# A two-layer streaming encoder in float32 products: the low part of weights split ahead of use is made by ScalarE and an accumulating DMA instead of VectorE

## The chip, the cores and the metric

The kernel runs on one core of a Trainium2 chip. Its time is the device time of one execution in microseconds (us). A core has five engines with a queue of their own: TensorE (PE, with PEld for loading its weights), VectorE (DVE), ScalarE (ACT), GpSimd (POOL), and SyncE (SP), which here only issues DMAs. Every engine works through its queue in order; waits between engines are semaphores.

## The reference

A trunk of two layers on 656 tokens (16 learned tokens, a prompt of 512, and 8 running streams of 16 tokens) with 1024 channels, all in float32. Cut to what matters here, one layer is:

```python
h = rmsnorm(x, g_mix)
proj = h @ w_in                      # then attention, convolution and a recurrence on its parts
x = x + mix @ w_out
h2 = rmsnorm(x, g_ffn)
gate, val = split(h2 @ w_up, 2)      # 1024 -> 2 x 2816
gate_c = causal_dwconv(gate, ffn_past, ffn_conv_w, ffn_conv_b)     # width 3
x = x + (gelu(gate_c) * val) @ w_down
```

After the second layer, `y = rmsnorm(x, g_final)` is written for all tokens, besides caches and states.

## The kernel before, in words

Activations lie with channels on the 128 partitions and tokens along the row; a block of 128 channels is one tile (`x0` to `x7`). A float32 product is made of three matmuls of a shorter type (float32r): every operand is split into a high part, which is the rounded value, and a low part, which is what the rounding left. `mm3` (L373) multiplies high by high, high weights by low activations, and low weights by high activations, into one accumulator.

Weights come from HBM into one of four buffers `raw` (up to 512 KB, 8 blocks of 128 rows; `w_load`, L342, a DMA on SP's queue). `w_split` cuts each half of such a buffer (256 KB, 128x512 elements) into its parts: ScalarE writes the high part (L359), VectorE subtracts it from `raw` and writes the low part (L360). Most units go through four shared buffers each, `whi` and `wlo`, which come free when TensorE has used them. Some weights are split ahead of their use, and their parts lie in tiles of their own, `ghi` and `glo` (argument `own`): 37 halves in the whole program. They are

- 3 halves for the first input projection at the very start (here `start["on"]` holds);
- in each layer, 6 halves for the first three blocks of the up-projection, split during the output projection (blocks `e_u`, written as `w3` below);
- in each layer, 4 halves for the first gates that are computed after those blocks (`wg`; their products are `d_g`, two blocks of output rows, each in two column ranges c0 and c1);
- 6 halves for the first blocks of layer 1's input projection, split at the end of layer 0;
- 8 halves for the last part of the last down-projection (`wl`; products `d_fin`), one for each block of 128 output rows, named m0 to m7 below. There the tokens are taken in two column ranges, 384 columns first and 256 columns after, so that the norm and the output of the first range overlap the products of the second. The first three halves are split at the start of the stage, that of m+3 when block m has been added to the residual.

Around the first gates the stage works as follows. ScalarE writes `ga`, the last tap of the short convolution (L1086), VectorE adds the other taps (L1089), ScalarE applies the gelu (L1092), GpSimd multiplies by the norm's factors (L1231, L1232), and VectorE multiplies the value product into it (`gv`, L1236 to L1238). GpSimd also copies rows of past gates into `gp` (L1076) and rows for the output into `gout` (L1081, L1082). After the first gates, pairs of blocks are multiplied by a Strassen scheme with seven products in place of eight: its sums of weights are `wcb` (GpSimd, L960), split into `whi` (ScalarE, L966) and `wlo` (VectorE, L967); its sums of activations are `fh` (ScalarE L1063, VectorE L1064); its products `d_v` and `d_g` are taken out by VectorE at L992 and L996.

The order on each engine is not that of the source: a recording layer collects the instructions and places them by a planner, so a change of one helper moves others too. The tile names in the profile are those in the program, without buffer numbers.

Of the kernel before, what the change touches and what calls it, by code (L numbers as in the profile page):

```python
# [9 lines left out]
F32 = mybir.dt.float32  # L10
# [3 lines left out]
ALU = mybir.AluOpType  # L14
# [142 lines left out]
def trunk_kernel(ctx: ExitStack, tc: tile.TileContext, i: dict, o: dict, depth: int = 2):  # L157
# [12 lines left out]
    V, A, G, PE = nc.vector, nc.scalar, nc.gpsimd, nc.tensor  # L170
# [148 lines left out]
    start = {"on": False}  # L319

    def seq(ins):

        if start["on"]:
            tc.keep_in_program_order(ins)
            start[ins.ins.engine] = ins.ins
# [19 lines left out]
    def unit_s(name):  # L345
        return S(name, F32R)[:, :512].rearrange("p (k n) -> p k n", n=128)

    def w_split(raw, kt, a=0, own=False):

        half = 4 if kt in (4, 8) else 3  # L350
        units = []
        while a < kt:
            n = min(half, kt - a)
            if own:
                hi, lo = unit_s("ghi"), unit_s("glo")
            else:
                hi = wsp.tile([128, 4, 128], F32R, tag="whi", name="whi")
                lo = wsp.tile([128, 4, 128], F32R, tag="wlo", name="wlo")
            seq(A.copy(hi[:, :n], raw[:, a:a + n]))  # L359
            seq(V.tensor_tensor(out=lo[:, :n], in0=raw[:, a:a + n], in1=hi[:, :n].bitcast(F32), op=ALU.subtract))  # L360
            units += [(hi, lo, m) for m in range(n)]
            a += n
        return units

    def weights(w, k0, kt, own=False):
        return w_split(w_load(w, k0, kt), kt, 0, own)
# [744 lines left out]
    for l in range(depth):  # L1111
# [7 lines left out]
        if l == 0:  # L1119
            hs = []  # L1120
            nc.sync.dma_start(out=xs[0][:, :T], in_=i["x"][0])
            raws = [w_load(w[col[n]], 0, 8, ((0, 4),)) for n in range(3)]
            for m in range(1, 4):
                nc.sync.dma_start(out=xs[m][:, :T], in_=i["x"][m])
            for n in range(3):
                nc.sync.dma_start(out=raws[n][:, 4:], in_=w[col[n], :, 512:].rearrange("p (k n) -> p k n", n=128))
            for m in range(4, 8):
                nc.sync.dma_start(out=xs[m][:, :T], in_=i["x"][m])
            w3 = []
            start["on"] = True  # L1130
            for m in range(8):
                hs.append(split(xs[m], par("g_mix", m), f"h{l}{m}"))
                if m == 0:
                    w3 = [w_split(raws[n], 4) for n in range(3)]
                if m == 3:
                    w3 = [w3[n] + w_split(raws[n], 8, 4, True) for n in range(3)]
            for m in range(8):
                sq_add(m, E=V)
            start["on"] = False
# [88 lines left out]
        for ft in range(2):  # L1228
            ps = ps3[2] if ft == 0 else gemm(weights(wu[NFF + 1], 0, 8), ks8, hs, f"v{l}1", cx, PB)
            a, av = gates.pop(ft)  # L1230
# [168 lines left out]
```

## Time and profile before

| | |
|---|---|
| median of 3 runs | 1700.11 us (1699.21 to 1701.23) |
| the profiled execution | 1700.97 us, of which the span from the first to the last instruction is 1699.2 us |
| mean granted TensorE clock | 0.988 of full speed |
| TensorE busy | 1626.8 us, 96% of the span |
| VectorE busy | 1288.1 us, 76% |
| ScalarE busy | 843.3 us, 50% |
| GpSimd busy | 552.7 us, 33% |
| transfers issued by GpSimd | 40, 13.44 MB, 4.5% of the 16 DMA engines' time |

The profile is of one execution. The busy shares are averages over stages with different limits; a stage is read from the timeline and from the waits that end last in it. An engine's idle time is put down to the engine or DMA whose signal came last.

### The profile page before, as it was taken

To read this page: it belongs to the slowest core of one execution; us is meant where nothing else is said; L and a number is where in the kernel's file an instruction comes from. 1 tells how busy PE (TensorE), PEld (TensorE's weight loads), DVE (VectorE), ACT (ScalarE), POOL (GpSimd) and SP (SyncE) were. 2 spreads that over 40 slices of the span, in tenths; PEclk is the share of its full clock that TensorE was granted. 3 is DMA by queue.
4 is the path that set the end of the run, shared out by engine and by line. 5 is a ranking of instruction groups with operands and counts; after the bars stand their busy time and mean duration, and the time that the engine had idled before them with its cause. 6 is when DMAs were issued, how large, how long until landed. Compare 5 with 4: busy or idle time off the path is not lost.

```text
span 1699.2 us, 28519 instructions
## 1 busy us (share of the span) xinstructions
PE 1626.8 (96%) x10772; PEld 1530.0 (90%) x10772; DVE 1288.1 (76%) x2470; ACT 843.3 (50%) x1648; POOL 552.7 (33%) x626
## 2 busy tenths in 40 slices
PE   7999999998989999999999999999999999999997
PEld 6898878898989999999988988788899899999996
DVE  6579985769896696696747898856899867768765
ACT  6656576554553343343427556665544434334334
POOL 0102220017563353462201032100276534435413
PEclk9999999999999999999999999999999999999998
DMA  6236431341213322222412364314502232222212
GB/s 221 77 92 158 115 98 42 105 163 70 75 66 113 109 81 84 74 74 86 158 64 86 94 149 99 93 57 135 177 29 75 88 118 83 96 67 80 88 49 87
DMA packets 68090, 164.62 MB, mean 97 GB/s; under 512 B 11984, under 2 KB 17616, under 8 KB 67952
## 3 DMA queue, kind: packets, MB, share of 16 engines
q1 hardware_dynamic: 62192, 149.36, 26.8%
q0 software_dynamic: 5760, 13.44, 4.5%
q8 instruction: 84, 1.38, 0.3%
q14 instruction: 54, 0.44, 0.1%
HBM read 129.80 MB, written 19.54 MB: 88 GB/s over the span
## 4 chain that ended last, share of the span: by engine, by line
PE 74%; DVE 16%; issue 4%; ACT 2%; POOL 2%; DMA 1%; SPq 0%; DVEq 0%; ACTq 0%; POOLq 0%
PE d_i L373 16%; PE d_dn L373 16%; PE d_v L373 10%; PE d_g L373 8%; PE d_oa L373 5%; DVE wlo L967 3%; DVE lo_g L332 2%; PE e_i L373 2%; PE e_u L373 2%; PE sc L490 2%; PE hl L784 1%; DVE ga L1089 1%; PE d_fin L373 1%; PE po L526 1%; DVE fh L1064 1%
## 5 line engine op out<-in xcount | busy, mean ns | idle before, releaser
L373 PE MATMUL d_v<-fh,whi 128*128 128x328 f32 (+1 forms) x1120 | 252.1, 312 | 1.3 <-ACT whi L966 1.3
L359 ACT CAST whi<-raw 128x384 fp32r<-128x384 f32 (+2 forms) x243 | 132.7, 548 | 239.7 <-PE d_i L373 76.4
L373 PE MATMUL d_g<-fh,whi 128*128 128x328 f32 (+1 forms) x1008 | 226.6, 312 | 0.0
L373 PE MATMUL d_i<-hi_h,whi 128*128 128x328 f32 x672 | 219.2, 326 | 0.0
L373 PE MATMUL d_i<-lo_h,whi 128*128 128x328 f32 x672 | 213.8, 318 | 0.0
L373 PE MATMUL d_i<-hi_h,wlo 128*128 128x328 f32 x672 | 212.8, 317 | 0.0
L373 PE MATMUL d_dn<-hi_g,wlo 128*128 128x328 f32 (+1 forms) x640 | 199.2, 312 | 6.1 <-DVE wlo L360 6.1
L373 PE MATMUL d_dn<-lo_g,whi 128*128 128x328 f32 (+1 forms) x640 | 199.0, 311 | 0.0
L373 PE MATMUL d_dn<-hi_g,whi 128*128 128x328 f32 (+1 forms) x640 | 198.4, 311 | 0.0
L360 DVE TENSOR_TENSOR wlo<-raw,whi 128x384 fp32r<-128x384 f32 (+2 forms) x243 | 164.3, 689 | 40.1 <-ACT whi L359 32.2
L373 PEld LDWEIGHTS d_v<-fh,whi 128*128 128x128 f32 x1120 | 189.2, 189 | 1.6 <-ACT whi L966 1.6
L373 PE MATMUL d_v<-fh,wlo 128*128 128x328 f32 (+1 forms) x560 | 176.5, 315 | 7.2 <-DVE wlo L967 6.5
L966 ACT CAST whi<-wcb 128x512 fp32r<-128x512 f32 x152 | 94.0, 619 | 164.1 <-PE d_dn L373 66.5
L373 PEld LDWEIGHTS d_g<-fh,whi 128*128 128x128 f32 x1008 | 170.2, 189 | 0.0
L373 PE MATMUL d_g<-fh,wlo 128*128 128x328 f32 (+1 forms) x504 | 158.3, 314 | 8.0 <-DVE wlo L967 8.0
L960 POOL TENSOR_TENSOR wcb<-raw 128x512 f32<-128x512 f32 x76 | 110.5, 1454 | 128.2 <-DMA raw<-in_w_up 71.9
L416 DVE TENSOR_TENSOR x<-d_dn,x 128x328 f32<-128x328 f32 (+1 forms) x112 | 55.2, 493 | 108.6 <-PE d_dn L373 107.2
L373 PEld LDWEIGHTS d_i<-hi_h,whi 128*128 128x128 f32 x672 | 127.3, 189 | 10.1 <-issue 5.6
L967 DVE TENSOR_TENSOR wlo<-wcb,whi 128x512 fp32r<-128x512 f32 x152 | 132.1, 869 | 4.4 <-ACT whi L966 3.7
L373 PEld LDWEIGHTS d_i<-lo_h,whi 128*128 128x128 f32 x672 | 127.5, 190 | 3.8 <-issue 1.3
L373 PEld LDWEIGHTS d_i<-hi_h,wlo 128*128 128x128 f32 x672 | 127.2, 189 | 3.0 <-issue 1.3
L373 PEld LDWEIGHTS d_dn<-hi_g,wlo 128*128 128x128 f32 x640 | 120.3, 188 | 7.7 <-DVE wlo L360 7.7
(387 smaller groups left out, 4090.3 us busy)
## 6 DMA issues: line engine op xcount, KB each, us to landing
raw<-in_w_up SPq DMA_DIRECT2D x88, 512.0 KB, 3.6
raw<-in_w_in SPq DMA_DIRECT2D x45, 512.0 KB, 3.8
raw<-in_w_down SPq DMA_DIRECT2D x48, 384.0 KB, 3.3
x_scr<-x SPq DMA_DIRECT2D x24, 328.0 KB, 2.9
x<-x_scr SPq DMA_DIRECT2D x24, 328.0 KB, 4.2
cvb<-cvt POOLq DMA_DIRECT2D x20, 328.0 KB, 5.1
cvd<-cvt POOLq DMA_DIRECT2D x20, 328.0 KB, 4.3
raw<-in_w_out SPq DMA_DIRECT2D x16, 384.0 KB, 3.2
```

The lines of the kernel that those rows point to most:

```text
L332: V.tensor_tensor(out=lo[:, a:T], in0=src[:, a:T], in1=hi[:, a:T].bitcast(F32), op=ALU.subtract)
L359: seq(A.copy(hi[:, :n], raw[:, a:a + n]))
L360: seq(V.tensor_tensor(out=lo[:, :n], in0=raw[:, a:a + n], in1=hi[:, :n].bitcast(F32), op=ALU.subtract))
L373: PE.matmul(ps[:, :b - a], lhsT=ww[:, n], rhs=r[:, a:b], start=first and j == 0, stop=last and j == 2)
L416: V.tensor_tensor(out=xs[m][:, a:b], in0=ps[c][:, :b - a], in1=xs[m][:, a:b], op=ALU.add)
L490: PE.matmul(ps[:, o0:o0 + w], lhsT=q[64 * c:64 * c + 64, q0:q0 + 128], rhs=k[64 * c:64 * c + 64, n * w:(n + 1) * w], start=True, stop=True)
L526: PE.matmul(po[:, :128], lhsT=vt[:, j * 128:(j + 1) * 128], rhs=aT[:, j * 128:(j + 1) * 128], start=j == 0, stop=False)
L784: PE.matmul(ps[:, c * 128:(c + 1) * 128], lhsT=kk[:, 16 + 128 * c:144 + 128 * c], rhs=both(m0 + 64 * c, 64), start=True, stop=True)
L960: G.tensor_tensor(out=t, in0=x, in1=y, op=op)
L966: A.copy(hi, x)
L967: V.tensor_tensor(out=lo, in0=x, in1=hi.bitcast(F32), op=ALU.subtract)
L1064: V.tensor_tensor(out=lo, in0=x, in1=hi.bitcast(F32), op=ALU.subtract)
```

## The change

For a half with a tile of its own, outside the very start, the low part is made in two steps. ScalarE writes the negative of the high part into `glo`, and a DMA that GpSimd issues adds the raw half to it. The diff:

```diff
             seq(A.copy(hi[:, :n], raw[:, a:a + n]))
-            seq(V.tensor_tensor(out=lo[:, :n], in0=raw[:, a:a + n], in1=hi[:, :n].bitcast(F32), op=ALU.subtract))
+            if own and not start["on"]:
+
+                A.mul(lo[:, :n], hi[:, :n].bitcast(F32), -1.0)
+                G.dma_start(out=lo[:, :n].bitcast(F32), in_=raw[:, a:a + n], accum_op=ALU.add)
+            else:
+                seq(V.tensor_tensor(out=lo[:, :n], in0=raw[:, a:a + n], in1=hi[:, :n].bitcast(F32), op=ALU.subtract))
```

It holds for 34 of the 37 halves: 12 of `w3`, 8 of `wg`, 6 at the end of layer 0 and 8 of `wl`. Lines of the changed kernel after line 360 have numbers that are 5 higher.

The instructions that follow in the program stand in another order too. At the first gates of layer 0, ScalarE's queue was, from the first `ghi` on (`ga_4555` and `ga_4568` are the two gates' tiles):

```order
L359 CAST ghi<-raw 128x512
L1086 ACTIVATE ga_4555<-gp_4547,cst 128x672
L1086 ACTIVATE ga_4568<-gp_4560,cst 128x672
L359 CAST ghi<-raw 128x512
L1092 ACT_TABLE_LOAD
L1092 ACTIVATE ga_4555<-ga_4555 128x672
L359 CAST ghi<-raw 128x512
L1092 ACTIVATE ga_4568<-ga_4568 128x672
```

and is now (the gates' tiles are `ga_4561` and `ga_4574`):

```order
L359 CAST ghi<-raw 128x512
L1091 ACTIVATE ga_4561<-gp_4553,cst 128x672
L362 ACTIVATE glo<-ghi 128x512
L1091 ACTIVATE ga_4574<-gp_4566,cst 128x672
L359 CAST ghi<-raw 128x512
L362 ACTIVATE glo<-ghi 128x512
L1097 ACT_TABLE_LOAD
L1097 ACTIVATE ga_4561<-ga_4561 128x672
L1097 ACTIVATE ga_4574<-ga_4574 128x672
```

Two writes of `glo` have come ahead of the load of the gelu's table, and the other two behind both gelus.

At the same place GpSimd's queue now reads as follows (`gp` and `gout` are the copies of rows, `ga<-ga,r_h` the products with the norm's factors):

```order
L1079 MEMSET gp_4725 128x2
L1081 COPY gp_4725<-gpast_4062 128x8x2
L363 DMA glo<-raw 128x512 x2
L1236 TENSOR_TENSOR ga_4561<-ga_4561,r_h_4333 128x528
L1237 TENSOR_TENSOR ga_4561<-ga_4561,r_h_4333 128x8x16
L1236 TENSOR_TENSOR ga_4574<-ga_4574,r_h_4333 128x528
L1237 TENSOR_TENSOR ga_4574<-ga_4574,r_h_4333 128x8x16
L363 DMA glo<-raw 128x512 x2
L1086 COPY gout_4496<-gp_4725 128x2
```

The two pairs of DMAs are new, one behind the copies and one behind the products with the norm's factors; what stood around them before is the same.

In the last stage TensorE's queue in the changed kernel, from the end of m2 on, is this (`d_fin03`, `d_fin04` and `d_fin05` are the accumulators of m3, m4 and m5 for the first 384 columns, `hi_g118` to `hi_g121` and `lo_g118` to `lo_g121` the activations' parts):

```order
L378 MATMUL d_fin03_18379<-hi_g118_18221,ghi_18322 128x384
L378 MATMUL d_fin03_18379<-lo_g118_18222,ghi_18322 128x384
L378 MATMUL d_fin04_18405<-hi_g118_18221,ghi_18348 128x384
L378 MATMUL d_fin04_18405<-lo_g118_18222,ghi_18348 128x384
L378 MATMUL d_fin03_18379<-hi_g118_18221,glo_18323 128x384
L378 MATMUL d_fin03_18379<-hi_g119_18265,ghi_18322 128x384
L378 MATMUL d_fin03_18379<-lo_g119_18266,ghi_18322 128x384
L378 MATMUL d_fin03_18379<-hi_g119_18265,glo_18323 128x384
```

Before, the twelve matmuls of a block stood together, but for one of m1. Now the first two of a later block, which need only `ghi`, stand ahead of the first that needs the earlier block's `glo`; this goes on to m7, and nine matmuls of m0's second column range stand ahead of m7's last ten. On VectorE, the addition of m3's second range (L1371 before) now stands ahead of the norm's last step (L316), and stood behind it.

## Rows read from the trace of the kernel before

**Rows 1.** The page, part 1 (busy time, share of the span and instructions of each engine) and part 4 (the chain of work that ended last, its share of the span by engine).

```profile
PE 1626.8 (96%) x10772; PEld 1530.0 (90%) x10772; DVE 1288.1 (76%) x2470; ACT 843.3 (50%) x1648; POOL 552.7 (33%) x626
...
PE 74%; DVE 16%; issue 4%; ACT 2%; POOL 2%; DMA 1%; SPq 0%; DVEq 0%; ACTq 0%; POOLq 0%
```

**Rows 2.** The view of one tile, for `glo` (first two rows) and for `ghi` (last row). A row of an instruction gives its count, its least, median and greatest duration in ns and the first and last start; the indented row says who waited for the instruction on line 360, with the sum in us and the number of times.

```profile
L360 DVE TENSOR_TENSOR glo<-raw,ghi x37: 672/684/1000, 11.4 to 1668.8; 128x512 fp32r<-128x512 f32 x37
...
  PE d_g L373: 4.7, 2
...
L359 ACT CAST ghi<-raw x37: 601/616/626, 10.5 to 1667.8; 128x512 fp32r<-128x512 f32 x37
```

**Rows 3.** The view of one line, L700, the only accumulating transfers of the kernel before (328 KB each, issued on POOL's queue). First row: how long POOL is held by one issue, in ns. The rows on landing give us from issue to landing, least, median and greatest: of the whole run, then of the one transfer issued between 134 and 135 us, of the three issued between 142 and 146 us, and of the three issued between 150 and 154 us.

```profile
L700 POOL DMA_DIRECT2D cvb<-cvt x20: 853/878/1864, 122.0 to 1059.9; - x20
...
DMA to landing us min/median/max: 3.6/4.7/7.3
...
DMA to landing us min/median/max: 3.7/3.7/3.7
...
DMA to landing us min/median/max: 3.7/4.6/5.4
...
DMA to landing us min/median/max: 4.2/5.5/6.6
```

**Rows 4.** TensorE at the first gates of layer 0: one row of the timeline (start us, duration us, instruction; in brackets the idle time before it and what ended it), and two stretches of 4 us from the view of windows (length; busy time and number of instructions of PE, PEld, DVE, ACT, POOL; granted clock; share of the DMA engines; GB/s).

```profile
423.44 0.64 PE L373 MATMUL d_g<-hi_h,glo 128*128 128x328 f32 x1 [2.38 <-DVE glo L360]
...
424.00:428.00 4.00, 4.00 (x20) 4.00 (x19) 3.26 (x6) 3.56 (x6) 2.63 (x2) 0.64 0.33 90
...
428.00:432.00 4.00, 4.00 (x29) 4.00 (x27) 3.25 (x9) 4.00 (x11) 2.82 (x4) 1.00 0.53 172
```

**Rows 5.** The timeline at the same place: ScalarE, then GpSimd, then VectorE. Columns as in the first row of rows 4.

```profile
420.89 0.95 ACT L1086 ACTIVATE ga<-gp,cst 128x672 f32<-128x672 f32 x1 [8.74 <-DVE gp L1222]
...
424.80 0.77 ACT L1092 ACTIVATE ga<-ga 128x672 f32<-128x672 f32 x1
...
423.43 0.85 POOL L1076 COPY gp<-gpast 128x16 f32<-128x16 f32 x1
...
425.65 2.62 POOL L1231 TENSOR_TENSOR ga<-ga,r_h 128x528 f32<-128x528 f32 x1 [1.37 <-ACT ga L1092]
...
422.71 0.68 DVE L360 TENSOR_TENSOR glo<-raw,ghi 128x512 fp32r<-128x512 f32 x1
...
430.45 0.50 DVE L1236 TENSOR_TENSOR gv<-d_v,ga 128x328 f32<-128x328 f32 x1 [0.75 <-POOL ga L1231]
...
433.39 0.49 DVE L1222 TENSOR_TENSOR gp<-d_g,r_h 128x328 f32<-128x328 f32 x1
```

**Rows 6.** The second part of the same stage, layer 0, 408 to 505 us. First two rows: TensorE's waits in that stretch (who waited for what: us in total, times, longest). Last two rows: the timeline of ScalarE and of VectorE.

```profile
PE d_v L373 <- DVE wlo L967: 2.2, 3, 1.3
...
PE d_v L373 <- ACT whi L966: 1.3, 1, 1.3
...
452.46 0.62 ACT L966 CAST whi<-wcb 128x512 fp32r<-128x512 f32 x1 [0.42 <-PE d_v L373]
...
463.57 1.24 DVE L967 TENSOR_TENSOR wlo<-wcb,whi 128x512 fp32r<-128x512 f32 x1 [1.83 <-ACT whi L966]
```

**Rows 7.** Busy time of each engine in us in the 64 us from 396 to 460, the sum row of the view of windows.

```profile
sum 64.00, PE 59.29 PEld 57.91 DVE 60.78 ACT 28.70 POOL 43.64; mean PE 14.82 PEld 14.48 DVE 15.20 ACT 7.18 POOL 10.91
```

**Rows 8.** The same place in layer 1, timeline of TensorE.

```profile
1258.42 0.41 PE L373 MATMUL d_g<-hi_h,glo 128*128 128x322 f32 x1 [2.29 <-DVE glo L360]
```

**Rows 9.** The two other early stages, from the timeline but for the second row, which is the view of the tile `glo` for TensorE between 350 and 400 us. First: VectorE at the end of layer 0's output projection. Third and fourth: ScalarE at the end of layer 0. Fifth and sixth: there, VectorE takes out the second column range of the fourth and of the fifth block of the last down-projection.

```profile
360.85 1.89 DVE L360 TENSOR_TENSOR glo<-raw,ghi 128x512 fp32r<-128x512 f32 x3
...
L373 PE MATMUL e_u<-hi_h,glo x20: 308/313/317, 388.4 to 399.8; 128*128 128x328 f32 x20
...
828.29 2.18 ACT L359 CAST ghi<-raw 128x512 fp32r<-128x512 f32 x4
...
833.82 0.62 ACT L359 CAST whi<-raw 128x512 fp32r<-128x512 f32 x1 [0.25 <-DVE glo L360]
...
843.53 0.48 DVE L416 TENSOR_TENSOR x<-d_dn,x 128x328 f32<-128x328 f32 x1
...
847.17 0.48 DVE L416 TENSOR_TENSOR x<-d_dn,x 128x328 f32<-128x328 f32 x1
```

**Rows 10.** The last stage, from the timeline: ScalarE (two rows), TensorE (one), VectorE (five). The rows of L1371 add the finished product of a block of 128 output rows to the residual: block 0, block 6, block 7. L316 and L1379 belong to the norm and the output of the first 384 token columns.

```profile
1646.90 1.66 ACT L359 CAST ghi<-raw 128x512 fp32r<-128x512 f32 x3
...
1659.52 0.61 ACT L359 CAST ghi<-raw 128x512 fp32r<-128x512 f32 x1
...
1655.93 0.44 PE L373 MATMUL d_fin<-hi_g,glo 128*128 128x384 f32 x1 [2.12 <-DVE glo L360]
...
1657.99 0.56 DVE L1371 TENSOR_TENSOR x<-d_fin,x 128x384 f32<-128x384 f32 x1 [0.91 <-PE d_fin L373]
...
1670.42 0.56 DVE L1371 TENSOR_TENSOR x<-d_fin,x 128x384 f32<-128x384 f32 x1 [0.95 <-PE d_fin L373]
...
1672.50 0.56 DVE L1371 TENSOR_TENSOR x<-d_fin,x 128x384 f32<-128x384 f32 x1 [1.52 <-PE d_fin L373]
...
1678.57 0.56 DVE L316 SCALAR_TENSOR_TENSOR r_fin<-rt_fin,r_fin 128x384 f32<-128x384 f32 x1
...
1679.38 5.50 DVE L1379 TENSOR_TENSOR y<-y,r_fin 128x384 f32<-128x384 f32 x6
```

## The prediction

> **What bounds the kernel now.** I read the page's busy times and its chain first: TensorE is busy 96% of the span and holds 74% of the chain, VectorE holds 16% [rows 1]. So the change can only move time where TensorE waits, or where it makes it wait. Then the view of the tile `glo`: a subtraction takes 0.68 us, and in the whole program TensorE waits for `glo` three times, 4.7 us in two waits at the first gates [rows 2] and 2.1 us once in the last stage [rows 10]. These 6.8 us are all that could be won directly. The subtractions also fill VectorE; where that engine is the limit, the slot of each, some 0.60 us since instructions there overlap by a little, may count. In the 64 us around the first gates VectorE is busy 60.78 us, more than TensorE with 59.29 [rows 7]. That is the one stage where this holds. I therefore cost four places apart.
>
> **What one new split costs.** The subtraction is replaced by a write on ScalarE, for which the nearest row is its copy of the same size, 0.62 us [rows 2], by an issue on GpSimd, 0.88 us in the median and up to 1.86 [rows 3], and by the landing of a DMA that adds 256 KB. The trace has only additions of 328 KB: 3.6 us at least, 4.7 in the median, 7.3 at most; one alone 3.7; three close together 3.7, 4.6, 5.4; three beside other traffic 4.2, 5.5, 6.6 [rows 3]. The DMAs here are smaller by a quarter, mostly single or in pairs, and some lie beside weight loads. I take 4.0 us for one, nearer the single ones than the median, and keep 7.3 and, below 3.6, 2.8 (3.6 x 256/328, as if all of it went with the size) for the range. A low part that was ready 0.7 us after the high one is now ready after about 0.6 + 0.9 and more, some 4.6 to 6 us in all where nothing else holds it.
>
> The Trainium skill, "DMA: Bandwidth & Descriptors", section "Anatomy of one DMA — SWDGE (gpsimd) path", gives about 2.0 us fixed plus bytes over 436 GB/s. For 328 KB that would be 2.8 us as an estimate, and the trace's least is 3.6, so the row decides. For 256 KB the page gives 2.6 us, with which the sum below would be about -1.4 in place of +4.
>
> **First blocks of the up-projection, both layers (12 halves).** In layer 0 VectorE writes the last three `glo` from 360.85 on, and TensorE first reads one at 388.4 [rows 9]. Six DMAs, even at 7.3 us, are over by some 375. VectorE and ScalarE have idle time there. The four raw buffers come free some us later, but the loads behind them are wanted later still. Cost: 0. The cover is the rest of the output projection; without it each half would cost its 4.6 us or more.
>
> **End of layer 0 (6 halves).** Four `ghi` start at 828.29 [rows 9]. Six writes of 0.62 put 3.7 us more on ScalarE, and the raw buffers are freed at landing: the second DMA is issued at about 830.5 and landed by 835, so the next load of `w_down` and its split end near 839, where `wlo` before was ready a little after 834.4 (its `whi` at 833.82). It is the unit of the fifth block, whose second column range VectorE takes out at 847.17, one block of 3.64 us after the fourth [rows 9], so TensorE reaches it near 842.5; 3 us are left. Cost: 0; with 7.3 us the cover is just used up.
>
> **First gates (4 halves in each layer).** Before, TensorE waited 2.38 us for the first `glo` and went on at 423.44; it then ran at a granted clock of 0.64 in the next 4 us, 20 matmuls in place of 29 [rows 4], which happens after this wait either way. In the changed order the first write stands behind the first `ga`, which ends at 421.84, so it is done at 422.5. But the DMA stands behind GpSimd's copies, the last of which ends at 423.43 + 0.85 = 424.28 [rows 5]. Landed at 424.28 + 4.0 = 428.3, it holds TensorE 4.85 us longer than before (3.7 at 2.8, 8.1 at 7.3). The second DMA, one issue later, lands about when its half is reached; the other pair has some 7 us.
>
> What is late next: the gate's first column range ends about 433.2, and VectorE takes it out in front of further `fh` (before at 433.39, without a wait [rows 5]). VectorE gains 4 x 0.60 = 2.4 us by the subtractions, so it is there near 432.0 and waits 1.2. The gelu at 424.80 moves by about 1 us through the two writes ahead of it, and with it GpSimd's product at 425.65; that takes most of the rest, since `gv` at 430.45 waits for it [rows 5]. So VectorE leaves the place about even, within 0.5 us of before.
>
> TensorE is 4.85 us late and finds waits to lose this in: 1.3 us for `whi` and 2.2 for `wlo` at `d_v` [rows 6], of which I put 1.8 at the first Strassen products (all of the 1.3, and one short wait for `wlo`). About 3.0 are left, and they couple back: ScalarE's next `whi` at 452.46 already waits for a buffer that TensorE must free, and VectorE waits for ScalarE behind it. VectorE has 1.83 us of idle time at 463.57 to absorb that [rows 6], which leaves 1.2; and GpSimd's sums of weights, which end that idle time, follow TensorE only in part. I take 0.9 us. Layer 1 has the same wait, 2.29 us to 1258.42 [rows 8], and the same copies ahead of the DMA: again 0.9. Bounds for each layer: -1.0 if VectorE's gain is kept and TensorE's lateness falls wholly into its waits, +3.0 if none of what is left is absorbed. Sum for both: +1.8.
>
> **Last stage (8 halves).** The first three are off VectorE, where they stood behind other work until TensorE went on at 1655.93 after 2.12 us. Now ScalarE alternates three copies and three writes from 1646.90 [rows 10], about 0.55 us from start to start; the DMAs go out at 1648.1, 1649.2 and 1650.3 and have landed by 1654.5. The first products then end earlier: m0 is added at about 1656.15 in place of 1657.99. From 1658.0 on the loop binds. From the addition of m to the start of the next `ghi` are 1659.52 - 1657.99 = 1.53 us [rows 10]; copy 0.53 and write 0.65 bring the issue to 2.7 us after the addition. With 4.0 us of landing and the block's last ten matmuls (2.08 us a block, from 1670.42 to 1672.50 [rows 10], so 0.174 each, 1.74) plus 0.05, m+3 is added 8.5 us after m, where three blocks took 6.25. In numbers: m0 1656.15, DMA of m3 at 1658.85, landed 1662.85, m3 added 1664.65; its DMA for m6 at 1667.35, landed 1671.35, m6 done 1673.1. For m1 the ScalarE queue puts a whole round (2.05 us) between the two DMAs: m4 landed 1664.85, added 1666.65, m7 issued 1669.4 behind m6's write, landed 1673.4, done 1675.15 in place of 1672.50: +2.65. Nine products of the second range (256 columns for 384, so two thirds of 0.174 us each) were done in the waits, about 1.05 us, so TensorE's next blocks are 1.6 late. But the norm's last step, at 1678.57 before [rows 10], now stands behind m3's second addition and comes 0.5 later for that, so the outputs start at 1681.5 rather than 1679.38, and from there to the end nothing is shorter: +2.2. Bounds: -0.6 at 2.8, +1.5 at 3.6, about +8 at 7.3 (the loop is passed twice, 3.3 each, plus what pairs cost).
>
> **Sum.** 0 + 0 + 1.8 + 2.2 = +4.0 on the profiled execution's 1700.97, so 1705.0; that execution lies 0.9 above the median of the runs, and on the median's scale it is 1700.11 + 4.0 = 1704.1. I say 1704.0. About 0.2%, 3.4 us, is what a measurement of this kernel can tell from no change, so the forecast is at that edge.
>
> **The rivals.**
> - *Hidden after all.* The landing is near 2.8 to 3.4 us. The loop of the last stage is then 7.3 to 7.9 us for three blocks, and two rounds of it cost 2.1 to 3.3, of which the 1.8 won at its start and the 1.05 of products done early pay most; TensorE is late by 3.6 to 4.2 at the gates and that is absorbed. Last stage -0.6 to +1, gates -0.4 each: 1698.7 to 1701. For it: smaller transfers, and the single one at 3.7. Against it: no row under 3.6. Chance 0.25.
> - *Faster.* VectorE is the limit from the gates on [rows 7], and what it is relieved of counts in full: 2.4 us in each layer less TensorE's unabsorbed part, and the last stage even. 1700.1 - 4 = 1696. It decides itself where VectorE takes out the first gate's columns: only if the landing is so short, about 2.8 us, that it doesn't wait there. Chance 0.10.
> - *Much slower.* GpSimd's issue grows towards 1.86 us and the landing towards 6 to 7 us, as weight loads start at the same time. Then 2.5 to 3 us in each layer, 5 to 7 in the last stage: 1710 to 1713. For it: 7.3 and 6.6 occur [rows 3]. Against it: the median is 4.7 for a larger transfer. Chance 0.17.
> - *The change is not on the path* in the two early stages is already my reading; that it is nowhere is excluded by the three waits of rows 2.
>
> **How the numbers follow.** The forecast, 1702 to 1706.5, has 0.48. It lies over 1703.5, which is 0.2% slower, in a little under two thirds. Slower: 0.48 x 0.63 + 0.17 = 0.47. Faster, under 1696.7: 0.10. Same: 0.43. The range goes from 1697.5 to 1711, which leaves out the faster case and the end of the much slower one.
>
> **What would show it.** In the profile after, TensorE's wait for `glo` at the first gates should be about 7 us in each layer with a DMA as its end, and no wait for `glo` at 1655. VectorE should wait about 1 us at the first `gp<-d_g`. In the last stage TensorE should have two or three waits of 1 to 2.5 us on DMAs between m2 and m7. The prediction is wrong if the additions land in under 3.3 or over 5.5 us, or if TensorE's lateness of 5 us is passed on through the `whi` buffers to the end of the stage.

## The result, and the profile after

The changed kernel is slower. Its median is 1712.96 us (1708.39 to 1713.65, four runs) against 1699.96 for the kernel before beside it: a ratio of 1.0065, with a 95% interval from 1.0053 to 1.0077, or +11.0 us. The two medians by themselves lie 13.0 us apart; this text goes by the ratio on record. One execution of a later kernel, the profiled one of experiment 12, ran in a slow state (1951.9 us, granted clock 0.75) and is left out. The forecast was +4 and the range ended at 1711. The direction was right, the size was not. The profiled execution has a span of 1710.9 us, 11.7 more than before.

From the page after: the busy times of the engines and the new transfers (count, KB each, median us to landing).

```profile
PE 1630.1 (95%) x10772; PEld 1535.0 (90%) x10772; DVE 1269.3 (74%) x2436; ACT 863.1 (50%) x1682; POOL 579.7 (34%) x660
...
glo<-raw POOLq DMA_DIRECT2D x34, 256.0 KB, 4.1
```

Against [rows 1], VectorE has lost 18.8 us of work, ScalarE gained 19.8 and GpSimd 27. TensorE's own work is 3.3 us longer with the same number of matmuls, so most of the 11.7 is idle time. Not all of it stands where the new operations are waited for. The view of the tile `glo` after (least, median and greatest duration in ns; then who waited, us and times; last the landing of its DMAs in us):

```profile
L362 ACT ACTIVATE glo<-ghi x34: 613/632/637, 355.4 to 1677.1; 128x512 fp32r<-128x512 f32 x34
L363 POOL DMA_DIRECT2D glo<-raw x34: 596/868/1180, 356.5 to 1678.2; - x34
...
  PE d_g L378: 11.1, 2
...
  PE d_fin L378: 3.0, 2
...
DMA to landing us min/median/max: 3.2/4.1/6.7
```

The write takes 0.63 us (0.62 was assumed), the issue 0.87 (0.88), the landing 3.2 to 6.7 with a median of 4.1 (4.0). TensorE waits for `glo` 14.1 us in place of 6.8 [rows 2, 10], but its other waits have changed too (TensorE's waits after: us in total, times, longest):

```profile
PE d_g L378 <- DMA glo<-raw: 11.1, 2, 6.0
...
PE d_ob L378 <- DVE x L421: 6.4, 4, 2.1
...
PE e_i L378 <- DVE x L421: 3.7, 1, 3.7
...
PE d_fin L378 <- DMA glo<-raw: 3.0, 2, 1.6
```

The wait of `e_i` for `x` did not exist before. It lies at the end of layer 0, where TensorE never waits for a new transfer. To see by stage where time goes, I matched the instructions of TensorE's queue in both traces and took the differences of their starts (medians around each place). A stage's cost is what the difference grows by in it:

| stage | difference on entry, on leaving | cost | forecast |
|---|---|---|---|
| first blocks of the up-projection, layer 0 | +0.3, +1.7 | +1.4 | 0 |
| gates and the rest of the feed-forward part, layer 0 | +1.7, +1.0 | -0.7 | +0.9 |
| end of layer 0 (to the first matmul of `np_h`) | +1.0, +7.1 | +6.1 | 0 |
| first blocks, layer 1 | +7.0, +7.2 | +0.2 | 0 |
| gates and the rest, layer 1 | +7.2, +6.6 | -0.6 | +0.9 |
| last stage | +6.6, +11.7 | +5.1 | +2.2 |

These are differences of one execution of each kernel, and they vary: in the traces of experiments 4 and 5, which leave the end of layer 0 as it is in the change, that stage costs 3.5 and 3.6 us.

**End of layer 0.** In the order SyncE (DMA issues; loads of `w_down` and `w_in`), ScalarE, VectorE, TensorE, all from the timeline after:

```profile
836.65 0.83 SPq L342 DMA_DIRECT2D raw<-in_w_down  x2
...
840.84 4.47 SPq L342 DMA_DIRECT2D raw<-in_w_down  x2
...
846.37 0.86 SPq L342 DMA_DIRECT2D raw<-in_w_in  x2
...
841.06 0.62 ACT L359 CAST whi<-raw 128x512 fp32r<-128x512 f32 x1 [2.77 <-DMA raw<-in_w_down]
...
854.36 0.62 ACT L359 CAST whi<-raw 128x512 fp32r<-128x512 f32 x1 [4.63 <-DMA raw<-in_w_in]
...
855.01 0.69 DVE L365 TENSOR_TENSOR wlo<-raw,whi 128x512 fp32r<-128x512 f32 x1 [3.15 <-ACT whi L359]
...
862.16 0.64 PE L378 MATMUL e_i<-hi_h,ghi 128*128 128x328 f32 x1 [3.69 <-DVE x L421]
...
867.52 2.55 PE L311 MATMUL np_h<-sq,onesd 128*128 128x328 f32 x4 [2.25 <-DVE sq L417]
```

and SyncE at the same place before:

```profile
832.36 2.97 SPq L342 DMA_DIRECT2D raw<-in_w_down  x3
...
836.02 2.15 SPq L342 DMA_DIRECT2D raw<-in_w_in  x2
```

The load for the fifth block of `w_down` was the last of a group of issues that ended at 831.08 before; now it is issued at 836.65, because SyncE waits until the new transfers let go of the buffers. SyncE's waits for them between 820 and 850 us (in the kernel before it has none of this kind):

```profile
SPq L342 <- DMA glo<-raw: 11.3, 3, 5.1
```

The cast of this block starts at 841.06, where it started at 833.82 [rows 9], and its subtraction is done at 842.40. TensorE's first product with the block, after and then before:

```profile
841.73 0.42 PE L378 MATMUL d_dn<-hi_g,whi 128*128 128x328 f32 x1 [1.07 <-ACT whi L359]
```

```profile
839.47 0.31 PE L373 MATMUL d_dn<-hi_g,whi 128*128 128x328 f32 x1
```

So TensorE itself waits for the late block. With two more waits, 0.16 and 0.46 us for `wlo` of this block and the next, and products behind the waits that take 0.42 us where they took 0.31, it leaves the blocks of `d_dn` some 2.5 us later, against the kernel before, than it entered the stage.

The other 3.6 us come at the wait for `x`. The three loads behind that of the fifth block were issued from 832.36 on before, and from 837.1 on now; the pair at 840.84 takes 4.47 us, since its second waits for a buffer. The loads of `w_in` follow ten us later than before (846.37, 836.02), and the first of them lands after 7.9 us where it landed after 5.0. ScalarE, whose queue is in order, stands at 854.36 after 4.63 us without work: it waited for a block of `w_in`, whose shared parts TensorE first uses at 889.45, and behind that instruction stand the squares and high parts of `x`. VectorE stands behind it in turn (3.15 us for `whi`), with its additions of `d_dn` into `x` behind that subtraction. So the accumulators come free late, TensorE waits 3.69 us for one, and the norm starts at 867.52 rather than 860.37. This second part is the one that varies: in the traces of experiments 4 and 5 the waits at the fifth block are the same, and that for `x` is 1.0.

**Last stage.** VectorE's additions of m0, m3 and m6, GpSimd's DMAs for m3 and m6, TensorE's first product that needs each, and one stretch of 4 us with its granted clock (columns as in [rows 4]):

```profile
1662.72 0.56 DVE L1376 TENSOR_TENSOR x<-d_fin,x 128x384 f32<-128x384 f32 x1 [0.85 <-PE d_fin L378]
...
1672.83 0.56 DVE L1376 TENSOR_TENSOR x<-d_fin,x 128x384 f32<-128x384 f32 x1 [6.07 <-PE d_fin L378]
...
1682.19 0.56 DVE L1376 TENSOR_TENSOR x<-d_fin,x 128x384 f32<-128x384 f32 x1 [4.39 <-PE d_fin L378]
...
1665.92 0.86 POOL L363 DMA_DIRECT2D glo<-raw  x1 [7.57 <-ACT sq L412]
...
1676.03 0.88 POOL L363 DMA_DIRECT2D glo<-raw  x1 [0.93 <-ACT glo L362]
...
1669.27 0.65 PE L378 MATMUL d_fin<-hi_g,glo 128*128 128x384 f32 x1 [1.65 <-DMA glo<-raw]
...
1680.14 0.44 PE L378 MATMUL d_fin<-hi_g,glo 128*128 128x384 f32 x1 [1.31 <-DMA glo<-raw]
...
1668.00:1672.00 4.00, 2.73 (x9) 2.73 (x10) 0.00 (x0) 1.67 (x4) 2.81 (x3) 0.67 0.85 167
```

The stage is entered 6.57 us late; less that, m0 is added at 1656.15, the very number of the forecast. From there a round of the loop takes 10.11 us (1662.72 to 1672.83) and then 9.36, where 8.5 were worked out.

**First gates.** TensorE goes on after its wait in layer 0, and in layer 1:

```profile
428.74 0.64 PE L378 MATMUL d_g<-hi_h,glo 128*128 128x328 f32 x1 [5.96 <-DMA glo<-raw]
...
1268.47 0.64 PE L378 MATMUL d_g<-hi_h,glo 128*128 128x322 f32 x1 [5.17 <-DMA glo<-raw]
```

The two waits are 3.6 and 2.9 us longer than before [rows 4, 8], and yet both stages end up a little shorter than before.

### The profile page after: what moved, and what is told of

Same layout as the page of the kernel before. It is cut to its first block, busy times and chain, and to the rows that moved or that the text cites. A ratio compares the mean times of both kernels' runs of the same rounds, so it can differ in the third digit from the quotient of the medians.

```text
span 1710.9 us, 28610 instructions
## 1 busy us (share of the span) xinstructions
PE 1630.1 (95%) x10772; PEld 1535.0 (90%) x10772; DVE 1269.3 (74%) x2436; ACT 863.1 (50%) x1682; POOL 579.7 (34%) x660
```

## The experiments

Three questions were open. *Is the loss at the end of layer 0 due to the held buffers (theory), or to the longer work of ScalarE, whose queue is where it shows (rival)?* *Do the gates cost or gain, taken alone?* *What in the last stage is the loop, and can it be broken?* In most edits the places are told apart by a name passed as `own` ("w3", "wg", "end", "wl") in place of `True`; the diffs show the line that decides. Each ratio is to the kernel before on the same chip, with its 95% interval, so gains are given by the difference of ratios.

### 1. End of layer 0 by VectorE again

```diff
-            if own and not start["on"]:
+            if own and own not in ('end',) and not start["on"]:
```

> The six halves at the end of layer 0 are subtracted by VectorE again, everything else is as in the change. By the two traces TensorE lost 6.3 us between 840 and 868 us. Theory 1 (the loss arises there, from these six halves): 5.5 to 6.5 us faster than the change, 1706 to 1707 us, ratio to the kernel before 1.0035 to 1.004. Rival (TensorE came to that place late and the stage only shows it, or the loss moves on to the next stage): less than 2 us is won, over 1711 us.

1.0026 [1.0017, 1.0035], median 1705.16: 6.6 us of the 11 are gone. The norm starts where it did before (TensorE, then SyncE):

```profile
860.17 2.56 PE L311 MATMUL np_h<-sq,onesd 128*128 128x328 f32 x4 [3.59 <-DVE sq L417]
...
832.20 2.80 SPq L342 DMA_DIRECT2D raw<-in_w_down  x3
```

The loss of the stage up to the norm hangs on its six halves, for none of whose transfers TensorE waits. By the two intervals the 6.6 us are uncertain by some 2.5 us either way.

### 2. End of layer 0: ScalarE's write stays, VectorE adds

```diff
-                G.dma_start(out=lo[:, :n].bitcast(F32), in_=raw[:, a:a + n], accum_op=ALU.add)
+                if own in ('end',):
+                    V.tensor_tensor(out=lo[:, :n], in0=raw[:, a:a + n], in1=lo[:, :n].bitcast(F32), op=ALU.add)
+                else:
+                    G.dma_start(out=lo[:, :n].bitcast(F32), in_=raw[:, a:a + n], accum_op=ALU.add)
```

> At the end of layer 0 ScalarE still writes minus the high part, six times, but VectorE adds the raw half in place of the DMA. Theory 1a (the loss is the raw buffers, which come free only when the DMAs have landed, so that later weight loads and what stands behind them in ScalarE's and VectorE's queues come late): the buffers come free about as before, the stage loses under 1.5 us, 1706 to 1708 us in all. Theory 1b (the loss is the 3.8 us of ScalarE's six writes): it stays, 1711 to 1713 us.

1.0041 [1.0027, 1.0055], median 1708.63, just above what was expected; its five runs go from 1704.5 to 1711.5, so the median says little. The trace says more: the norm starts at 861.85,

```profile
861.85 2.56 PE L311 MATMUL np_h<-sq,onesd 128*128 128x328 f32 x4 [3.59 <-DVE sq L420]
```

1.5 us later than before, of which 1.1 came with it into the stage. So in this execution the stage costs 0.4 us with ScalarE's six writes and without the transfers. By the trace the rival falls; by the medians alone it would keep up to 2.5 us (1.0041 against 1.0026).

### 3. A fifth raw buffer

```diff
-NR = 4
+NR = 5
-NSLOT = 57
+NSLOT = 56
```

> The change with five raw buffers instead of four (and 56 slots instead of 57, to make room). If the losses at the first blocks and at the end of layer 0 come from raw buffers that are held until the landing: the shift of TensorE between 800 and 868 us, +6.3 us in the change and about +0.6 us with VectorE's addition, falls to under 2.5 us, and the whole to 1703 to 1708 us. If it comes from the order of ScalarE's queue alone: over 4 us of shift there, over 1709 us.

This keeps the whole change and gives it one more `raw` (and one of the general slots less, to make room). 1.0033 [1.0021, 1.0045], median 1707.52. At the end of layer 0 (SyncE, ScalarE, TensorE):

```profile
840.29 1.11 SPq L342 DMA_DIRECT2D raw<-in_w_in  x2
...
846.70 0.62 ACT L359 CAST whi<-raw 128x512 fp32r<-128x512 f32 x1 [0.73 <-DMA raw<-in_w_in]
...
860.83 2.56 PE L311 MATMUL np_h<-sq,onesd 128*128 128x328 f32 x4 [2.53 <-DVE sq L417]
```

The loads of `w_in` start at 840.29, six us sooner, ScalarE waits 0.73 us for one where it waited 4.63, and the norm starts at 860.83: the stage, entered about 2 us late, is left 0.46 late and costs nothing, although the landings there were slower than in the change (median 5.9 against 5.0 us between 820 and 850). With experiments 1 and 2 this settles the first question: it is the time for which an adding transfer holds its source buffer. The fifth buffer is no cure for the rest: at the first blocks this order loses 3.2 us in layer 0 and 3.3 in layer 1, among others by a wait of 1.87 us for `x` at 392.80 (0.40 in the change), and the last stage is nearly as slow as in the change (+4.5).

### 4. Last stage by VectorE again

```diff
-            if own and not start["on"]:
+            if own and own not in ('wl',) and not start["on"]:
```

> The eight halves of the last stage are subtracted by VectorE again, everything else is as in the change. By the two traces the last stage lost 5.1 us. If that comes from these halves: 1707.5 to 1708.5 us, ratio 1.0045 to 1.005. If the last stage would lose a part anyway, since it is entered late or since the clock falls there for another reason: over 1710 us.

1.0037 [1.0024, 1.0051], median 1708.09: 4.8 us back, about what the table's +5.1 says.

### 5. The change with four blocks ahead in the last stage

```diff
-WA = 2
+WA = 4
```

> The change as it is, but in the last stage four halves instead of two are asked for ahead of the loop over the blocks (WA = 4), so that five low parts stand in ScalarE's queue ahead of the first block's squares, and m+5 is split when m is added. Theory 3 (the last stage loses 5.1 us because the way from one addition over ScalarE's two writes, GpSimd's issue and the landing to the products of three blocks on is 8 us against 6.25 us, and because the clock falls in the waits): the waits on DMAs between m2 and m7 go, the stage ends 1 to 2 us earlier than before, in all 1705.5 to 1708 us. Rival (the stage is slow since the DMAs lie beside weight loads, however far ahead): over 1710.5 us.

`WA` is how many blocks' weights are split ahead when the stage starts, and how far ahead of the addition the next is asked for. 1.0017 [1.0008, 1.0025], median 1703.81: 8 us back, more than was expected. The additions of m0 and m7 and TensorE's only wait for a `glo` there:

```profile
1660.49 0.56 DVE L1376 TENSOR_TENSOR x<-d_fin,x 128x384 f32<-128x384 f32 x1 [0.85 <-PE d_fin L378]
...
1675.09 0.56 DVE L1376 TENSOR_TENSOR x<-d_fin,x 128x384 f32<-128x384 f32 x1 [1.54 <-PE d_fin L378]
...
1666.76 0.44 PE L378 MATMUL d_fin<-hi_g,glo 128*128 128x384 f32 x1 [0.37 <-DMA glo<-raw]
```

From m0 to m7 it now takes 14.60 us; before it was 14.51 (1657.99 to 1672.50) and in the change 21.56 (1662.72 to 1684.28). With the loop opened, the stage keeps what the forecast saw at its start and is 2.5 us shorter than before.

### 6. The kernel before with four blocks ahead

```diff
-WA = 2
+WA = 4
```

> The kernel before with four halves asked for ahead in the last stage, all subtracted by VectorE: the control for the run beside it. VectorE then has five subtractions between the last down-projection and the first products. If the gain in the last stage is the early DMAs: ratio 0.9995 to 1.001. If it is only the splits being ahead: ratio 0.998 to 0.999.

1.000 [0.9991, 1.0009]. Splitting further ahead gives nothing by itself: TensorE still waits for VectorE's first `glo` there:

```profile
1659.17 0.44 PE L373 MATMUL d_fin<-hi_g,glo 128*128 128x384 f32 x1 [2.12 <-DVE glo L360]
```

So the 2.5 us that the stage gains in experiment 5's one trace come from taking the first splits off VectorE, not from asking for splits sooner.

### 7. The gates alone

```diff
-            if own and not start["on"]:
+            if own and own not in ('end', 'wl', 'w3') and not start["on"]:
```

> Only the eight halves of the first gates go by ScalarE and DMA, all others are subtracted by VectorE. Theory 2 (there VectorE's relief is worth more than TensorE's longer wait: the two traces show -0.8 and -0.6 us over the two up-projections): 1698 to 1699.5 us, ratio 0.999 to 1.000. Rival, as the prediction had it: the wait of 5 us is passed on in part, +1.8 us, 1701.5 to 1702 us, ratio 1.001. TensorE's wait for the DMA at the gates should be 5 to 6 us in each layer either way.

0.998 [0.9971, 0.9989], median 1698.25: 3.4 us faster than before. TensorE's waits between 405 and 505 us, here,

```profile
PE d_g L378 <- DMA glo<-raw: 5.3, 1, 5.3
...
PE d_v L378 <- DVE wlo L972: 0.4, 1, 0.4
```

and VectorE's in the change in the same stretch:

```profile
DVE gp L1227 <- PE d_g L378: 1.0, 1, 1.0
```

TensorE waits 5.3 us for the transfer, and the waits of [rows 6] for `wlo` and `whi` shrink from 3.5 to 0.4. In the traces the stage is 2.0 us shorter in layer 0 and 1.4 in layer 1. The low part is ready later than before (TensorE waits 5.3 us for it, and 2.4 before [rows 4]), so the gain cannot be an earlier low part; what is left is that VectorE has less to do.

### 8 and 9. The gates' splits asked for sooner, by DMA and by VectorE

In both, the same line is moved to before the sums of activations; in the first on top of experiment 7, in the second in the kernel before:

```diff
+        wg = [weights(wu[ft], 0, 8, True) for ft in range(2, 2 + NPG)]
         fac = factors(l, r, cx)
...
-        wg = [weights(wu[ft], 0, 8, True) for ft in range(2, 2 + NPG)]
```

> Only the first gates go by ScalarE and DMA, and their splits are asked for before the sums of activations, so that the four DMAs stand ahead of most of GpSimd's sums and of the copies. TensorE's wait of 5.3 and 5.0 us for the DMA at the gates, and the 2.4 us of the kernel before, should be gone. If TensorE's waits there count: 2 to 5 us faster than with the gates alone, 1693.5 to 1696.5 us, ratio 0.996 to 0.998. If they fall into later waits, since VectorE sets the end of the stage: 1697 to 1698.5 us, ratio 0.998.

> The kernel before, with the splits of the first gates asked for before the sums of activations, as in the run beside it, but subtracted by VectorE. It tells what the place alone is worth. If the gain at the gates is VectorE's relief: 1699.5 to 1702 us, ratio 0.999 to 1.001. If it is the earlier low part: 1695 to 1697.5 us, ratio 0.997 to 0.998.

1.0031 [1.0019, 1.0044] and 1.0024 [1.0014, 1.0034]: both slower, against what I expected of either. TensorE now waits for VectorE's `gp` at the blocks of gates (the first of two in layer 0), by DMA and then by VectorE:

```profile
423.75 0.61 PE L378 MATMUL d_g<-hi_h,ghi 128*128 128x328 f32 x1 [3.81 <-DVE gp L1228]
```

```profile
422.92 0.39 PE L373 MATMUL d_g<-hi_h,ghi 128*128 128x328 f32 x1 [2.94 <-DVE gp L1223]
```

The wait for `glo` is gone, and `gp` is late instead. In experiment 9 four subtractions now stand among the sums that VectorE has to do first, and what is wanted earlier displaces them. In experiment 8 VectorE does no subtraction there, and yet its sums of activations take longer (least, median and greatest ns of the eight of layer 0):

```profile
L1047 DVE SCALAR_TENSOR_TENSOR x<-x,cst,r_h x8: 1524/1530/4801, 398.7 to 412.8; 128x656 f32<-128x656 f32 x8
```

The one that starts at 403.75 took 4.80 us, and in it GpSimd issued its fourth new transfer (405.39); in experiment 7 the greatest is 1.93. Why VectorE is held there was not tested. These two runs thus do not show what an earlier low part alone would be worth.

### 10. The first blocks of the up-projection alone

```diff
-            if own and not start["on"]:
+            if own and own not in ('end', 'wl', 'wg') and not start["on"]:
```

> Only the twelve halves of the first blocks of the up-projection go by ScalarE and DMA. If the effects of the four places add, what is left for this one is 11 - 6.6 - 4.8 + 3.2 = +2.8 us: 1703.5 to 1705 us, ratio 1.0012 to 1.002. If it is hidden, as the prediction had it: ratio 0.9995 to 1.0005.

1.0018 [1.0009, 1.0026], median 1704.03: about 3 us slower. It is the chain of the end of layer 0 again (SyncE, ScalarE, VectorE, TensorE, layer 0; then SyncE before):

```profile
353.60 7.04 SPq L342 DMA_DIRECT2D raw<-in_w_up  x2
360.73 14.20 SPq L342 DMA_DIRECT2D raw<-in_w_out  x7
...
365.11 0.62 ACT L359 CAST ghi<-raw 128x512 fp32r<-128x512 f32 x1 [2.74 <-DMA raw<-in_w_up]
...
367.24 0.42 DVE L365 TENSOR_TENSOR wlo<-raw,whi 128x256 fp32r<-128x256 f32 x1 [3.28 <-ACT whi L359]
...
379.88 0.39 PE L378 MATMUL d_ob<-hi_mx,whi 128*128 128x328 f32 x1 [3.15 <-DVE x L421]
```

```profile
355.23 1.57 SPq L342 DMA_DIRECT2D raw<-in_w_up  x2
360.96 10.74 SPq L342 DMA_DIRECT2D raw<-in_w_out  x7
```

Two loads of `w_up` take 7.04 us to issue where they took 1.57, the seven of `w_out` behind them 14.20 for 10.74; ScalarE waits for the late block, VectorE behind it, and TensorE waits 3.15 us for `x`. The change has the same late loads.

### 11. All 34 halves: ScalarE's write stays, VectorE adds

The edit of experiment 2 with `own in ('end', 'wl', 'w3', 'wg')`.

> At all four places ScalarE writes minus the high part, as in the change, but VectorE adds the raw half in place of the DMA. It parts the DMA from ScalarE's write. Theory 1a extended (the losses at the first blocks, at the end of layer 0 and in the last stage are landings: raw buffers held, and the loop of the last stage): the three losses of 2.8, 6.6 and 4.8 us shrink to under 1 us each, and the gain at the gates, which is VectorE's relief, is gone too: 1700.5 to 1703 us, ratio 1.000 to 1.0015. Rival (ScalarE's 0.63 us for each half is what is lost): 1706 to 1710 us.

1.0018 [1.0008, 1.0027], median 1704.47, a little above the range expected. The transfers are thus worth 8 us of the 11 (1.0065 less 1.0018). At most 3 us are left for the writes, which here have VectorE's additions behind them. The trace does not show them at the three places where the change loses (first blocks 0.0, end of layer 0 +0.3, last stage 0.0); there the gates cost +0.1 and +1.1, since VectorE has its work back.

### 12. What gains, together

```diff
-WA = 2
+WA = 4
-            if own and not start["on"]:
+            if own and own not in ('end', 'w3') and not start["on"]:
```

> ScalarE and DMA only at the first gates (there worth 3.2 us) and in the last stage, with four halves asked for ahead (WA = 4); VectorE subtracts at the first blocks and at the end of layer 0. In the run with four halves ahead the last stage ended 2.5 us earlier than before, against where it was entered. If the two add: -5.7 us, 1695 to 1696.5 us, ratio 0.996 to 0.9975. If not: no better than the gates alone, ratio 0.998 or more.

0.9966 [0.9954, 0.9978], median 1696.11: 5.8 us faster than before, and 16.8 faster than the change. The gains of experiments 5 and 7 add up. Its trace is not used.

## Why the prediction was right or wrong

The parts measured apart add up to the whole: first blocks +3 (experiment 10), gates -3.4 (7), end of layer 0 +6.6 (1), last stage +4.8 (4), together +11.0, which is what the change costs. That it comes out so exactly is luck: each part is uncertain by 1.5 to 3 us, and two of them are what a part costs alone, two what is gained by leaving it out. In the profiled execution they are +1.6, -1.3, +6.1 and +5.1.

**The cost of one split: right.** Write, issue and landing came out at 0.63, 0.87 and 4.1 us. The Trainium skill, "DMA: Bandwidth & Descriptors", section "Anatomy of one DMA — SWDGE (gpsimd) path", would give 2.6 us for 256 KB as an estimate; the trace's least is 3.2 and its median 4.1, so the row of the larger transfers was the better guide here too.

**End of layer 0: the step that failed most, 0 against +6.1.** I followed one buffer to the next load of `w_down` and compared the end of its split, 839, with when TensorE reaches *that* block, 842.5: "3 us are left". Both times were wrong. The split was done at 842.40, for the load was issued at 836.65, behind transfers that SyncE waited 11.3 us for. And TensorE had reached the block at 839.47 in the kernel before: 842.5 was read off VectorE, which takes a block out some 4 us after TensorE has finished it. So there was no slack, and TensorE waited 1.07, 0.16 and 0.46 us at the late blocks and lost, with slower products behind these waits, some 2.5 us in all. The rest, 3.6 us here and 1.0 in two other traces, was not looked at. The buffers are a ring: six halves that hold three of four buffers some 3 us longer delay every load behind them, and the `w_in` loads came ten us later. The cast of a late block stands in ScalarE's queue ahead of work that is due now, and VectorE's additions stand behind that. For such a cast the slack is that of the next instruction in its queue. The sentence "with 7.3 us the cover is just used up" put the danger into a slow landing; landings there were 4.0 to 6.7 us with a median of 5.0, and the cover was used up by the number of loads that wait for a buffer.

**First blocks: 0 against +1.4 to +3.** Wrong by the same ring of buffers and the queues behind it: "the loads behind them are wanted later still" was a look at TensorE's need, not at SyncE's and ScalarE's queues. In layer 1 the 0 held (+0.2).

**First gates: the places right, the sign wrong (+0.9 a layer against -0.7 and -0.6, and -2.0 and -1.4 alone).** TensorE went on at 428.74; less the 1.67 us by which the stage is entered late, that is 427.1 (428.3 forecast, the issue coming 0.5 us and the product 0.7 us sooner than assumed). VectorE waited 1.0 us for `d_g` (1.2 forecast, in part by luck: 433.39 less 2.4 of relief is 431.0, not 432.0), and the waits for `wlo` and `whi` took up the lateness as described. What failed is the last step, "couple back": of 3.0 us left I let 0.9 be passed on. Instead nothing was, and VectorE's relief, put at 2.4 us, was kept in part. The row for it was there: this is the stage in which VectorE was busier than TensorE [rows 7]. This is the mechanism of the faster rival without its condition of a short landing.

**Last stage: mechanism right, size +5.1 against +2.2.** A round was put at 8.5 us. In the first, the DMA was issued 3.20 us after the addition (2.70 assumed: ScalarE's chain was 0.1 longer, and 0.40 passed between the end of the write and the issue, which I had left out); the product began 3.35 us after the issue (4.0 assumed); and the block's last ten products took 3.56 us to the addition in place of 1.79, since in this execution TensorE's granted clock fell to 0.67 behind the wait. 0.50 - 0.65 + 1.77 is the 1.6 by which the round was longer. In the second round issue, landing and products were 3.20, 4.11 and 2.05: +0.9. These 2.5 us pass on to m7, which is added 2.6 us later than worked out, and are most of the 2.9 by which the stage was mis-sized. The clock's fall had been seen at the gates [rows 4] and was not put into this sum. It does not come in every execution: in experiment 1, whose last stage has the same instructions, TensorE's wait is as long and the clock stays at 1.00 (its product, then a stretch as above):

```profile
1662.81 0.45 PE L378 MATMUL d_fin<-hi_g,glo 128*128 128x384 f32 x1 [1.61 <-DMA glo<-raw]
...
1664.00:1668.00 4.00, 3.94 (x21) 3.19 (x19) 1.11 (x2) 2.34 (x5) 1.57 (x2) 1.00 0.74 149
```

There the first round takes 8.56 us, as forecast, the second 9.04, and the stage costs +3.2; in experiment 2 it costs +3.6. So without the clock's fall the sum is 1.0 to 1.4 us short; the rest of the miss came with the clock.

**The rivals and the range.** "Much slower" had the right total for a wrong reason: not slow issues and landings on the waits for `glo`, but late loads where no one waits for `glo`. The range was too narrow because two stages were set to 0 without a bound.

## What to carry to other kernels

A transfer that takes over an engine's work also holds that work's source buffer until it lands, so count its cost in the ring of buffers and in every in-order queue behind the next load, not only at the consumer of its result. Take the time when a consumer needs a block from the consumer's own queue, not from an engine that works behind it. Moving work off an engine pays where that engine is the busiest of its stage and the result is asked for far enough ahead (gates, and the last stage with four blocks ahead: 5.8 us together); inside a loop of short rounds its latency is paid in every round. When a stage is costed at 0, write down which instruction stands next in each queue behind the one that gets later.

## What the runs showed of the hardware

- A short wait can cost more than its length, but the same wait does not always. In the change, waits of 0.48 and 1.65 us in the last stage were followed by a granted clock of 0.67 (1668 to 1672), and a block took 1.77 us longer; in experiment 1, waits of 0.48 and 1.61 us at the same place were followed by 1.00. One wait of 2.12 us was followed by 1.00 in the kernel before [rows 10] and by 0.57 in experiment 6 (1660 to 1664). What decides it was not settled here.
- Runs of one kernel differ along with their mean clock: three of the change at 0.984 took 1712.9 to 1713.7 us, the one at 0.988 took 1708.4. A single profile may show either.
- While GpSimd issued a new transfer, one sum on VectorE took 4.80 us in place of 1.53 (experiment 8); the cause was not tested.
- Adding transfers of 256 KB landed in 3.2 us at best, though single plain loads of 512 KB have a median of 3.6 on the page after.
